# Values of the 16 leading tokens in one layer of a hybrid decoder: from float32 operands, in four column tiles of the array

## The chip, the cores and the metric

The kernel runs on one core of one Trainium2 chip. The metric is the device time of the whole program in microseconds (us), as the median of some runs. A core has a matrix engine (TensorE, PE in the profile), three engines for elementwise work (VectorE or DVE, ScalarE or ACT, GpSimd or POOL), and SyncE (SP), which here only issues transfers. The engines run side by side, each through its own queue in order, and wait for each other on semaphores. Matmul results go to PSUM, which has eight banks.

## What is computed

One layer over 1024 tokens with 16 learned leading tokens (the "meta tokens") ahead of them. One projection of the normed input feeds two groups of heads, a gated delta rule (four heads, in chunks) and softmax attention with a forget gate (eight heads of 64 columns); then come an output projection and a feed-forward block. Cut to what matters:

```python
h = jnp.concatenate([meta, x], axis=1)          # 16 + 1024 tokens
u = rmsnorm(h, attn_norm_w[l])
proj = u @ w_in[l]
gq, gk, gv, gz, gb, ga, fq, fk, fv, ff = jnp.split(proj, IN_SPLITS, axis=-1)
o_gdn = gated_deltanet_group(...)               # gq, gk, gv, gz, gb, ga
o_fox = forgetting_attention_group(fq, fk, fv, ff, fgate_b[l])
h = h + jnp.concatenate([o_gdn, o_fox], axis=-1) @ w_out[l]
h = h + swiglu(rmsnorm(h, ffn_norm_w[l]), w_gate[l], w_up[l], w_down[l])
```

The change touches the rows of `fv` (the attention's values, 512 columns) and `ff` (its eight gate columns) that belong to the 16 leading tokens.

## The kernel before

A float32 product is made of three matmuls in a faster format. `split` (L162 to L165) casts a float32 tile to a high part on ACT (L163) and takes the rest as a low part on DVE (L164); each 128 rows of the contraction are then high by high, high by low and low by high. The normed input lies transposed as `uh` and `ul` (eight slices of 128 channels, 1040 token columns, the leading tokens in the first 16). `win_block` loads a block of the input projection's weights in two halves of four slices each (the raw tile from a pool of two buffers, `wraw`, issued by SP at L175) and splits each half into high and low (from a pool of four buffers each).

PE's order is written out by hand, by `PeOrder` (`od`). Chains of dependent steps, such as `levels` (inverses of the delta rule's triangular blocks), `scan` with its chunks, `csum` and the attention, yield the time at which their next step may come, in a modelled clock `od.t`, which each step advances by what it is charged (`od.pe`). When no chain is due, `od.run` takes one matmul from the fill, a generator: first `fox` (the gate block z0; the values `fv` in two halves of the heads, b=1 and then b=0; the keys `fk`; the queries `fq`), and when that has run out, the first part of the output projection, `wog`. What a fill matmul is charged is its column count divided by 2400. The other engines' queues and SP's are ordered by a scheduler, which simulates the program.

In `fox`, the values take one tile of 128 tokens after another: 24 matmuls through `proj_tmg` into a PSUM bank (three banks take turns, `ps_mm`), then the split into a tile `fvt` (three buffers) with the cast on ACT and the rest on DVE, then a store to `v_d` by SP (L878); for b=1 the eight gate columns are copied to `fr` as well (L881). The 16 leading tokens are the first tile of each half, t=-1: 24 matmuls with 16 stationary columns, `uh` or `ul` of these tokens, and 264 (b=1) or 256 (b=0) weight columns streaming.

While the first half of the values runs, the last delta-rule head is prepared: PE transposes its key norms `rk` (prk, L466 and L467), which come from POOL (L463); DVE copies the row out, SP stores it (L471, L472) and loads it back on all partitions (rkr, L474); DVE and POOL scale the blocks `ktna` (L498 to L502); SP stores them (L504), loads them transposed (`ad`, L543), DVE inverts 32x32 blocks (`up`, L533 and L535) and they go back to memory; `levels` loads the inverses (`ubk`) and copies them into `u` (L610, half on ACT).

At the scan's end each of eight chunks ends in products `po` (L789, L790); ACT copies them to `oc` (L793) and squares them; DVE and POOL make the norm; DVE scales (`on`, L808); PE transposes (`ot`, L814) and `split` writes it for the output projection. Then the attention begins: SP loads for each head its keys and queries (`ka`, `qa`, `kk`, `sa`, L937 to L945) and values (`avt`, L947), and PE makes scores (`sc`, L975 and L976). The memory of these tiles is in part what the scan held until `on` was done.

Of the kernel before, what the change touches and what calls it, by code (L numbers as in the profile page):

```python
# [9 lines left out]
F32 = mybir.dt.float32  # L10
F32R = mybir.dt.float32r
# [4 lines left out]
P = 128  # L16
D = 1024
KT = D // P
NM = 16
S = 1024  # L20
T = NM + S
NT = S // P
GH = 4
FH = 8
DH = 64
# [72 lines left out]
def tile_hymba_layer(ctx, tc, x, meta, attn_norm_w, w_in, conv_w, a_log, dt_bias, gdn_norm_w,  # L98
                     fgate_b, w_out, ffn_norm_w, w_gate, w_up, w_down, final_norm_w, out):
    nc = tc.nc  # L100
# [13 lines left out]
    def ps_mm(name):  # L114
        rot[0] = rot[0] % 3 + 1 if rot[0] else 0
        return ps_v(name) if rot[0] > 1 else bank("mm", 1, name)
# [35 lines left out]
    v_d = dram.tile([FH, T, P], F32, name="v_d")  # L152
# [9 lines left out]
    def split(dst_hi, dst_lo, src):  # L162
        cast = nc.scalar.copy(dst_hi, src)  # L163
        tail[0] = (cast, nc.vector.tensor_sub(dst_lo, src, dst_hi.bitcast(F32)))  # L164
        return cast  # L165

    def load_w(parts, name, hl=None):
        n = sum(m for _, m in parts)
        raw = wraw.tile([P, WMAX], F32, tag="raw", name=f"raw_{name}")
        o = 0  # L170
        for src, m in parts:
            d = raw[:, o:o + m]
            if len(src.shape) == 3:
                d = d.rearrange("p (k c) -> p k c", k=src.shape[1])
            nc.sync.dma_start(d, src)  # L175
            o += m
        hi, lo = hl or (wsp.tile([P, WMAX], F32R, tag=f"w{c}", name=f"w{c}_{name}") for c in ("hi", "lo"))
        for a in range(0, n, n // parts_n[0]):
            b = min(n, a + n // parts_n[0])
            split(hi[:, a:b], lo[:, a:b], raw[:, a:b])  # L180
        return hi, lo

    parts_n = [1]

    def win_block(c0, n, name):
        ws = ([], [])
# [60 lines left out]
    def norm_to(src, rows, wb, hi, lo, col, pool, nm):  # L247
        junk = pool.tile([P, D], F32, tag="junk", name=f"jk_{nm}")
        st = pool.tile([P, 4], F32, tag="st", name=f"st_{nm}")
        with tc.issue_after(casts[-2][0].ins) if len(casts) > 2 else nullcontext():  # L250
            nc.scalar.activation(junk[:rows], src[:rows], AF.Square, accum_out=st[:rows, 0:1])
        pows.append(inv_rms(st[:rows, 2:3], st[:rows, 0:1], 1, 1.0 / D, st[:rows, 1:2]))
        xn = pool.tile([P, D], F32, tag="xn", name=f"xn_{nm}")
        nc.vector.scalar_tensor_tensor(xn[:rows], src[:rows], st[:rows, 2:3], wb[:rows],
                                       op0=ALU.mult, op1=ALU.mult)
        for g in range(2):
            pt = ps_t(f"pt_{nm}_{g}")
            pv = pt.rearrange("p (a b) -> p a b", a=4)[:, :, :rows]
            for i in range(4):
                k = 4 * g + i  # L260
                nc.tensor.transpose(pv[:, i, :], xn[:rows, P * k:P * k + P], ident[:rows, :rows])
            split_dst = (hi[:, 4 * g:4 * g + 4, col:col + rows], lo[:, 4 * g:4 * g + 4, col:col + rows])
            split(split_dst[0], split_dst[1], pv)
        casts.append(tail[0])

    def tok_cols(t):
# [9 lines left out]
    def proj_fm(w, m0, c0, n, name):  # L276
# [2 lines left out]
                          uh[:, k, c0:c0 + n], ul[:, k, c0:c0 + n]) for k in range(KT)])  # L279
        return acc  # L280

    gt = gpool.tile([P, NT + 1, 8], F32, name="gt")
    fr = gpool.tile([P, NT + 1, FH], F32, name="fr")
    nc.gpsimd.memset(gt[:, NT], 0.0)
# [399 lines left out]
    def proj_tmg(acc, t, w, n):  # L684
# [5 lines left out]

    fox_ws = [(GZ, 256, "z0"), (FV + 256, 264, "fv1"), (FV, 256, "fv0"), (FK, 256, "fk0"), (FK + 256, 256, "fk1"),
              (FQ, 256, "fq0"), (FQ + 256, 256, "fq1")]
    fox_w = []

    def fox_load():
        if fox_ws:
            fox_w.append(win_block(*fox_ws.pop(0)))

    def fox_proj(dst, chunks, off, scale, nm):
        for b in range(2):  # L700
# [156 lines left out]
    def fox():  # L857
        fox_load()
        w = fox_w.pop(0)
        for t in range(NT):  # L860
            if t == 1:
                fox_load()
            acc = ps_mm(f"z0_{t}")
            yield from proj_tmg(acc, t, w, 256)
            gate_out(t, acc, fvp, "fvt", 0)
        for b in (1, 0):
            n = 256 + 8 * b
            w = fox_w.pop(0)
            for t in range(-1, NT):
                if t == 1:  # L870
                    fox_load()
                col, rows = tok_cols(t)
                acc = ps_mm(f"fv{b}_{t}")
                yield from proj_tmg(acc, t, w, n)
                vt = fvp.tile([P, 4, 2, DH], F32R, tag="fvt", name=f"fvt{b}_{t}")
                av = acc[:rows, :256].rearrange("p (h d) -> p h d", d=DH)
                split(vt[:rows, :, 0], vt[:rows, :, 1], av)
                nc.sync.dma_start(v_d[4 * b:4 * b + 4, col:col + rows].rearrange("h t d -> t h d"),  # L878
                                  vt[:rows].rearrange("p h a d -> p h (a d)").bitcast(F32))
                if b:  # L880
                    nc.vector.tensor_copy(fr[:rows, NT if t < 0 else t], acc[:rows, 256:264])  # L881
        fvc.close()
        yield from fox_proj(lambda m: k_d[m], TCH, 0, 1.0, "fk")
        od.add(csum(), od.t + 8.0)
        yield from fox_proj(lambda m: q_d[m].rearrange("a p c -> p a c"), ((NM, 342), (NM + 342, 342), (NM + 684, 340)), NM, -DH ** -0.5, "fq")
# [778 lines left out]
```

## Time and profile before

| what | value |
|---|---|
| median of 3 runs | 1319.92 us (1317.76, 1319.92, 1321.94) |
| profiled execution | 1319.71 us, with a span of 1318.0 us |
| mean granted TensorE clock | 0.997 of full |
| values' first half, leading tokens (24 matmuls) | from 235.61 us |
| values' second half, leading tokens (24 matmuls) | from 268.98 us |
| last chunk's products end | 443.79 us |
| first attention scores | 459.99 us |

The profile shows one execution. A line of PE reads: start, duration, engine, line, operation, output <- inputs, shape of the stationary and the streaming operand, count, and in brackets idle time ahead of it with what ended it. In a list of waits the columns are total, times and the longest. A chain of waits goes back from the last instruction through what released each piece.

### The profile page before, as it was taken

Reading aid. Unit: us, or ns where it says so; the run is one execution under the profiler, and the core shown is the slowest. Engines: PE = TensorE matmul, PEld = TensorE weight load, DVE = VectorE, ACT = ScalarE, POOL = GpSimd, SP = SyncE. Lnnn points to the kernel's source line nnn. Section 1 sums busy time; section 2 is a strip of 40 time slices with the busy share of each in tenths; the row PEclk is TensorE's granted clock in tenths of the full one; section 3 lists DMA queues with packets and bytes.
Section 4 is the critical chain, followed back from the end, with each engine's and each line's share of the span. In section 5 each row is a group of like instructions: output and inputs, shape, how many; then the busy total and the mean of one; then the engine's idle time right before and its main releaser. Section 6 shows DMA issues by size and latency. Waiting matters only on the chain.

```text
span 1318.0 us, 20035 instructions
## 1 busy us (share of the span) xinstructions
PE 1294.8 (98%) x7442; PEld 1133.6 (86%) x7442; DVE 855.3 (65%) x1526; ACT 545.4 (41%) x918; POOL 390.8 (30%) x348
## 2 busy tenths in 40 slices
PE   8999999999999999999999999999999999999998
PEld 8999999899999988887777888888888888888887
DVE  6665789676337578996897665566566565355645
ACT  5543434232223367885553232333333343343332
POOL 2211423601013311113432644554334453010301
PEclk9999999999999999999999999999999999999999
DMA  6331743774479597647534555534444557955523
GB/s 227 100 100 45 207 140 112 203 225 148 144 235 323 185 250 219 163 115 228 171 133 137 186 176 184 160 133 157 157 165 155 176 194 264 405 183 180 209 74 128
DMA packets 184776, 233.88 MB, mean 177 GB/s; under 512 B 19120, under 2 KB 136872, under 8 KB 181864
## 3 DMA queue, kind: packets, MB, share of 16 engines
q1 hardware_dynamic: 181704, 223.70, 52.8%
q0 software_dynamic: 2976, 8.92, 2.3%
q8 instruction: 58, 0.95, 0.3%
q14 instruction: 38, 0.31, 0.1%
HBM read 154.91 MB, written 77.67 MB: 176 GB/s over the span
## 4 chain that ended last, share of the span: by engine, by line
PE 74%; DVE 9%; DMA 7%; issue 3%; ACT 3%; SPq 2%; POOL 1%; POOLq 0%; DVEq 0%; ACTq 0%
PE xp L1545 9%; PE yp L1545 7%; PE gb L1379 5%; PE ud L1379 5%; PE gd L1379 5%; PE ub L1379 5%; PE ga L1379 4%; PE ua L1379 4%; PE pj_fk L207 4%; PE pj_fq L207 3%; PE ue L1379 2%; PE ge L1379 2%; PE fv L207 2%; PE pt L1012 2%; PE po L1034 1%
## 5 line engine op out<-in xcount | busy, mean ns | idle before, releaser
L164 DVE TENSOR_TENSOR al_p<-ra_p,ah_p 128x2048 fp32r<-128x2048 f32 (+1 forms) x21 | 46.7, 2222 | 93.7 <-ACT ah_p L163 93.7
L163 ACT CAST ah_p<-ra_p 128x2048 fp32r<-128x2048 f32 (+1 forms) x21 | 37.1, 1766 | 105.8 <-PE xp L1545 48.5
L1545 PE MATMUL xp<-wh_p,al_p 128*128 128x512 f32 (+1 forms) x176 | 67.3, 382 | 0.0
L1545 PE MATMUL xp<-wl_p,ah_p 128*128 128x512 f32 (+1 forms) x176 | 67.3, 382 | 0.0
L1545 PE MATMUL xp<-wh_p,ah_p 128*128 128x512 f32 (+1 forms) x176 | 67.3, 382 | 0.0
L1432 POOL TENSOR_TENSOR gzw<-gzw,uzt 128x512 f32<-128x512 f32 x11 | 18.4, 1673 | 154.9 <-DVE uzt L1423 128.9
L1432 POOL TENSOR_TENSOR gxy<-gxy,uxy 128x512 f32<-128x512 f32 x22 | 38.9, 1766 | 66.1 <-DVE uxy L1423 45.8
L985 ACT ACTIVATE pr<-pr,sm 128x144 f32<-128x144 f32 (+3 forms) x64 | 50.5, 790 | 17.7 <-DVE sm L980 17.4
L1379 PE MATMUL gb<-uh_p,w_g_p 128*128 128x512 f32 x176 | 57.8, 389 | 0.0
L1379 PE MATMUL gd<-uh_p,w_g_p 128*128 128x512 f32 x176 | 57.8, 389 | 0.0
L1379 PE MATMUL ud<-uh_p,w_u_p 128*128 128x512 f32 x176 | 57.8, 389 | 0.0
L1379 PE MATMUL ub<-uh_p,w_u_p 128*128 128x512 f32 x176 | 57.8, 389 | 0.0
L164 DVE TENSOR_TENSOR w_u_p<-raw_u,w_u_p 128x512 fp32r<-128x512 f32 x42 | 42.8, 1018 | 21.6 <-ACT w_u_p L163 21.5
L164 DVE TENSOR_TENSOR pl<-pt,ph 128x512 fp32r<-128x512 f32 (+1 forms) x96 | 51.1, 553 | 2.2 <-ACT ph L163 1.6
L1379 PE MATMUL ga<-uh_p,w_g_p 128*128 128x512 f32 x160 | 52.5, 389 | 0.0
L1379 PE MATMUL ua<-uh_p,w_u_p 128*128 128x512 f32 x160 | 52.5, 389 | 0.0
L1545 PE MATMUL yp<-wh_p,ah_p 128*128 128x512 f32 x132 | 51.3, 389 | 0.0
L1545 PE MATMUL yp<-wl_p,ah_p 128*128 128x512 f32 x132 | 51.3, 389 | 0.0
L1545 PE MATMUL yp<-wh_p,al_p 128*128 128x512 f32 x132 | 51.3, 389 | 0.0
L163 ACT CAST ph<-pt 128x512 fp32r<-128x512 f32 (+1 forms) x96 | 44.9, 471 | 13.8 <-PE pt L1012 13.3
L164 DVE TENSOR_TENSOR wl_p<-rw_p,wh_p 128x2048 fp32r<-128x2048 f32 (+1 forms) x21 | 46.9, 2236 | 3.4 <-ACT wh_p L163 3.4
L163 ACT CAST w_u_p<-raw_u 128x512 fp32r<-128x512 f32 x42 | 26.1, 620 | 52.3 <-PE gd L1379 33.6
(646 smaller groups left out, 4305.4 us busy)
## 6 DMA issues: line engine op xcount, KB each, us to landing
ra_p<-ao_p SPq DMA_DIRECT2D x14, 1024.0 KB
raw_g<-in_w_gate_dram SPq DMA_DIRECT2D x22, 512.0 KB
raw_u<-in_w_up_dram SPq DMA_DIRECT2D x22, 512.0 KB
raw_d<-in_w_down_dram SPq DMA_DIRECT2D x22, 512.0 KB
wt_p<-raw_d SPq DMA_DIRECT2D x33, 256.0 KB
rw_p<-wt_p SPq DMA_DIRECT2D x8, 1024.0 KB
rw_p<-in_w_down_dram SPq DMA_DIRECT2D x6, 1024.0 KB
ao_p<-gzw SPq DMA_DIRECT2D x22, 256.0 KB
```

What stands on the lines that cost most here:

```text
L163: cast = nc.scalar.copy(dst_hi, src)
L164: tail[0] = (cast, nc.vector.tensor_sub(dst_lo, src, dst_hi.bitcast(F32)))
L207: nc.tensor.matmul(dst, a, b, start=first, stop=last)
L985: nc.scalar.activation(pr[:, :n], pr[:, :n], AF.Exp, bias=sm[:, np_ - 1:np_], scale=-1.0, accum_out=rsum[:, h, j:j + 1])
L1012: nc.tensor.transpose(pt[:rows_k, P * j:P * j + P], pts[j][0][:, c0:c0 + rows_k], ident)
L1034: nc.tensor.matmul(po[:, q], vt[:, kt], pl[:, q], start=False, stop=(kt == nk - 1))
L1379: nc.tensor.matmul(dst, a[:, c], b[:, k], start=(first and k == 0 and i == 0), stop=(k == 3 and i == 2), skip_group_check=not first)
L1432: last_mul[0] = G.tensor_tensor(gs[d], gs[d], us[d], op=ALU.mult)
L1545: nc.tensor.matmul(dst[:, n_], a[:, f, c], b[:, f, n_], start=(first and i == 0 and n == 0), stop=(i == NF - 1 and n == 2), skip_group_che ...
```

## The change

The leading tokens' values no longer use the split operands. While the input is normed, a float32 copy of the transposed leading tokens is kept in `xm` (128 channels, eight slices, 32 columns, of which 16 are filled and the rest are zero). A new generator, `fv_meta`, makes the block of each half of the heads ahead of the other tiles: for each of the eight slices, four float32 matmuls with the 32 columns of `xm` stationary and 64 raw weight columns streaming, one for each head, each in its own 32-column tile of the array (`tile_position=(0, 32 * j)`), so that a head's 16 rows come out on partitions 32j to 32j+15. For b=1 the tile j=0 takes 72 columns: its head's and the eight gate columns. The planner is charged 0.12 us for each slice. The result is split as a 128x64 tile, and four stores take the place of one. The weights are read from the raw tiles, so `fox_load` keeps them (`fox_raw`), and the raw tiles are held until `fv_meta` has read them.

```diff
@@ load_w
+        raws_in[:] = [*raws_in[-1:], raw]
         return hi, lo
@@ norm_to
             split(split_dst[0], split_dst[1], pv)
+            if rows < P:
+                nc.vector.tensor_copy(xm[:, 4 * g:4 * g + 4, :rows], pv)
...
+    xm = gpool.tile([P, KT, 32], F32, name="xm")
+    nc.gpsimd.memset(xm, 0.0)
...
+            fox_raw.append(list(raws_in))
+
+    def fv_meta(b, raws):
+        n = 256 + 8 * b
+        acc = ps_mm(f"fvm{b}")
+        for k in range(KT):
+            w = raws[k // 4][:, n * (k % 4):n * (k % 4) + n]
+            for j in range(4):
+                c0, m = (192, n - 192) if j == 0 else (64 * j - 64, 64)
+                nc.tensor.matmul(acc[32 * j:32 * j + 32, :m], xm[:, k], w[:, c0:c0 + m], start=(k == 0),
+                                 stop=(k == KT - 1), tile_position=(0, 32 * j))
+            od.pe(0.12)
+            yield
+        vt = fvp.tile([P, 4, 2, DH], F32R, tag="fvt", name=f"fvmt{b}")
+        split(vt[:, 0, 0], vt[:, 0, 1], acc[:, :DH])
+        for j in range(4):
+            nc.sync.dma_start(v_d[4 * b + (j + 3) % 4, 0:NM],
+                              vt[32 * j:32 * j + NM, 0].rearrange("p a d -> p (a d)").bitcast(F32))
+        if b:
+            nc.vector.tensor_copy(fr[:NM, NT], acc[:NM, DH:DH + 8])
@@ fox
-            for t in range(-1, NT):
+            yield from fv_meta(b, fox_raw[1 if b else 2])
+            for t in range(NT):
...
-                    nc.vector.tensor_copy(fr[:rows, NT if t < 0 else t], acc[:rows, 256:264])
+                    nc.vector.tensor_copy(fr[:rows, t], acc[:rows, 256:264])
```

The change moves instructions beside the block. PE around the transpose prk, where the first half's block ends; before (fv_-1 is the old block, fv_0 the next tile of 128 tokens, tr_v transposes of the delta rule's values):

```order
L207 MATMUL fv_-1_2795<-whi_fv_1_2588,uh 16x264
L207 MATMUL fv_-1_2795<-wlo_fv_1_2589,uh 16x264
L207 MATMUL fv_-1_2795<-whi_fv_1_2588,ul 16x264
L466 MATMUL prk_2326<-ident,rk 8x128
L467 MATMUL prk_2326<-ident,rk 1x16
L437 MATMUL tr_v_0_2382<-ident,vt_1611 128x128 x4
L437 MATMUL tr_v_1_2387<-ident,vt_1611 128x128 x4
L207 MATMUL fv_0_2825<-whi_fv_0_2582,uh 128x264
```

and now (fvm is the new block):

```order
L712 MATMUL fvm_2799<-raw_fv_1_2590,xm 32x64 x2
L471 MATMUL prk_2330<-ident,rk 8x128
L472 MATMUL prk_2330<-ident,rk 1x16
L442 MATMUL tr_v_0_2386<-ident,vt_1615 128x128 x4
L442 MATMUL tr_v_1_2391<-ident,vt_1615 128x128 x4
L712 MATMUL fvm_2799<-raw_fv_1_2590,xm 32x64
L712 MATMUL fvm_2799<-raw_fv_1_2590,xm 32x72
L712 MATMUL fvm_2799<-raw_fv_1_2590,xm 32x64 x3
L208 MATMUL fv_0_2840<-whi_fv_0_2586,uh 128x264
```

The last 5 of the block's 32 matmuls come behind prk and tr_v. (In the changed kernel's own numbering a line is one higher up to L264 of the old, then up to 26 higher.)

ACT in the values' first half, up to the second half's first tiles; before:

```order
L163 CAST fvt_5_3012<-fv_5_2987 128x4x64
L610 COPY u_3364<-ubk_3359 32x16x32
L163 CAST fvt_6_3042<-fv_6_3017 128x4x64
L610 COPY u_3364<-ubk_3359 32x16x32
L163 CAST whi_fk_0_3137<-raw_fk_0_3135 128x1024
L163 CAST fvt_7_3072<-fv_7_3047 128x4x64
L163 CAST whi_fk_1_3143<-raw_fk_1_3141 128x1024
L163 CAST fvt_-1_3102<-fv_-1_3077 16x4x64
```

and now, from three tiles earlier:

```order
L163 CAST fvt_2_2937<-fv_2_2912 128x4x64
L163 CAST whi_fv_0_2872<-raw_fv_0_2870 128x1024
L163 CAST whi_fv_1_2878<-raw_fv_1_2876 128x1024
L163 CAST fvt_3_2967<-fv_3_2942 128x4x64
L163 CAST fvt_4_2997<-fv_4_2972 128x4x64
L163 CAST fvt_5_3027<-fv_5_3002 128x4x64
L163 CAST fvt_6_3057<-fv_6_3032 128x4x64
L615 COPY u_3430<-ubk_3425 32x16x32 x2
L163 CAST fvt_7_3087<-fv_7_3062 128x4x64
L163 CAST fvmt_3125<-fvm_3092 128x64
```

The cast of fvt_6 stands ahead of both copies of `ubk`; the casts of the second half's weights (raw_fv), which stood ahead of the whole first half, are behind fvt_2, and the casts of fk's weights have gone further back. On SP the loads of raw_fv, which were issued long before, stand behind the store of the first half's fvt_0, and raw_fk's first load, which stood there, behind that of fvt_6; the store of the last gate tile (zt_7, L303) stood ahead of the rk row's store (L471) and is now behind `mkv`'s.

DVE at the scan's end; before (on_4936 is the last chunk's output, wlo_wo low parts of the output projection's weights, ul_p the split of a transposed chunk):

```order
L803 TENSOR_TENSOR os_4930<-os_4930,rq_2487 128x4
L212 TENSOR_SCALAR os_4930<-os_4930 128x4
L164 TENSOR_TENSOR ul_p_4148<-ot_4947,uh_p_4146 128x4x128
L805 TENSOR_TENSOR os_4930<-os_4930,rq 128x4
L808 SCALAR_TENSOR_TENSOR on_4936<-oc_4919,os_4930,zt_4851 128x128 x4
L715 SCALAR_TENSOR_TENSOR fhl_fq_358_4963<-pj_fq_358_4907,fhl_fq_358_4963 128x342
L164 TENSOR_TENSOR wlo_wo_10_5799<-raw_wo_10_5796,whi_wo_10_5798 128x512 x2
L164 TENSOR_TENSOR wlo_wo_11_5807<-raw_wo_11_5804,whi_wo_11_5806 128x512 x2
```

and now (on_4990):

```order
L828 TENSOR_TENSOR os_4984<-os_4984,rq_2491 128x4
L164 TENSOR_TENSOR wlo_wo_10_5825<-raw_wo_10_5822,whi_wo_10_5824 128x512
L213 TENSOR_SCALAR os_4984<-os_4984 128x4
L164 TENSOR_TENSOR wlo_wo_10_5825<-raw_wo_10_5822,whi_wo_10_5824 128x512
L164 TENSOR_TENSOR ul_p_4202<-ot_5001,uh_p_4200 128x4x128
L830 TENSOR_TENSOR os_4984<-os_4984,rq 128x4
L164 TENSOR_TENSOR wlo_wo_11_5833<-raw_wo_11_5830,whi_wo_11_5832 128x512
L833 SCALAR_TENSOR_TENSOR on_4990<-oc_4973,os_4984,zt_4905 128x128 x4
L164 TENSOR_TENSOR wlo_wo_11_5833<-raw_wo_11_5830,whi_wo_11_5832 128x512
```

Three of the four wlo_wo casts stand ahead of `on`. They need buffers of the query weights, which are free when fq's last matmuls have read them. On PE at this place, behind the last chunk's products `po`, stood 13 pj_fq, ot of chunk 6, 32 pj_fq, ot of chunk 7, one pj_fq and 36 wog ahead of the first scores; now 13 pj_fq, ot of chunk 6, 10 pj_fq, ot of chunk 7 and 36 wog. On SP one load of raw_wo has moved ahead of the first attention head's loads, and the store of the last-but-one fq tile, which stood behind the first of these loads, ahead of them too.

More of the change, by code (lines that the diff above doesn't have):

```diff
@@ L180, in load_w @@
             split(hi[:, a:b], lo[:, a:b], raw[:, a:b])
+        raws_in[:] = [*raws_in[-1:], raw]
         return hi, lo
-    parts_n = [1]
+    parts_n, raws_in = [1], []
     def win_block(c0, n, name):
@@ L692, in tile_hymba_layer @@
               (FQ, 256, "fq0"), (FQ + 256, 256, "fq1")]
-    fox_w = []
+    fox_w, fox_raw = [], []
     def fox_load():
```

## The prediction

> **What bounds the kernel now.** I read the page first, then what TensorE (PE) waited for, and then the chain that ended last, around the two places where those waits lie. The profiled execution took 1319.71 us: a span of 1318.0 and 1.71 around it. The runs shown have their median at 1319.92, so the profiled one stands for them, and shifts are added to 1319.71. Busy time and the chain by engine, from the page:
>
> ```profile
> PE 1294.8 (98%) x7442; PEld 1133.6 (86%) x7442; DVE 855.3 (65%) x1526; ACT 545.4 (41%) x918; POOL 390.8 (30%) x348
> ...
> PE 74%; DVE 9%; DMA 7%; issue 3%; ACT 3%; SPq 2%; POOL 1%; POOLq 0%; DVEq 0%; ACTq 0%
> ```
>
> PE is busy nearly all the time, but a quarter of the chain is other engines' work: PE work counts only where PE is what is late. PE's waits between 180 and 480 us, longest first:
>
> ```profile
> PE prk L466 <- POOL rk L463: 2.0, 1, 2.0
> PE fv L207 <- DVE up L535: 1.7, 1, 1.7
> PE sc L975 <- DMA qa<-c_d: 1.0, 1, 1.0
> ```
>
> The two blocks that the change replaces stand exactly ahead of the first two waits. PE in order of time (start, duration, shape, and in brackets the wait ahead of it):
>
> ```profile
> 235.61 0.28 PE L207 MATMUL fv_-1_2795<-whi_fv,uh 128*16 128x264 f32 x1
> ...
> 238.38 0.28 PE L207 MATMUL fv_-1_2795<-whi_fv,ul 128*16 128x264 f32 x1
> 240.62 0.27 PE L466 MATMUL prk<-ident,rk 128*8 128x128 f32 x1 [1.96 <-POOL rk L463]
> ...
> 271.62 0.28 PE L207 MATMUL fv_-1_3077<-whi_fv,ul 128*16 128x256 f32 x1
> 273.59 0.36 PE L207 MATMUL fv<-whi_fv,uh 128*128 128x256 f32 x1 [1.69 <-DVE up L535]
> ```
>
> From 240.62 to 271.90 PE works without a wait and still comes 1.69 us too early. So in this stretch PE is not the bound. The chain of waits says what is (start, duration, piece):
>
> ```profile
> 257.83 2.38 POOL ktna L502
> ...
> 261.83 2.67 DMA ad_d<-ktna
> ...
> 265.43 4.59 DMA ad<-ad_d
> ```
>
> That is the preparation of the last delta-rule head: PE's next piece, at 273.59, needs a PSUM bank, which the cast of tile fvt_6 gives back; and on ScalarE (ACT) that cast stands behind a copy at L610 that waits for the end of this preparation:
>
> ```profile
> 271.48 0.62 ACT L610 COPY u<-ubk 32x512 f32<-32x512 f32 x1 [7.37 <-DMA ubk<-ud_d]
> 272.12 0.37 ACT L163 CAST fvt<-fv 128x256 fp32r<-128x256 f32 x1
> ```
>
> From 273.59 on the chain is PE, up to the end of the scan. There it leaves PE again:
>
> ```profile
> 443.79 2.05 PE pj_fq L207 x13
> ...
> 447.99 0.88 DVE on L808 x3
> ...
> 465.31 9.44 DMA ka<-k_d
> ```
>
> The last chunk's output `on` is ready at 447.99+0.88 = 448.87; right after it the loads of the attention heads begin, and head 1's scores wait for them at 476.15:
>
> ```profile
> 451.08 0.60 PE L814 MATMUL ot<-ident,on 128*128 128x128 f32 x4
> ...
> 459.99 0.23 PE L975 MATMUL sc<-ka,qa 70*128 70x144 f32 x1
> ...
> 476.15 0.30 PE L975 MATMUL sc<-ka,qa 70*128 70x144 f32 x1 [0.99 <-DMA qa<-c_d]
> ```
>
> **The change, part by part.**
>
> *The blocks themselves.* Removed: two blocks of 24 matmuls, (238.38−235.61)/23 = 0.120 us apart, 2.9 us each. Added: 32 float32 matmuls each. The trace has float32 matmuls at array positions already: L619 issues 32 for a pair of heads and the trace records 64, so each runs as two passes, and a block has 64. Their pace, from 32 columns and 64 columns (durations of one are min/median/max in ns):
>
> ```profile
> 306.07 2.11 PE L619 MATMUL py<-u,na 32*32 32x32 f32 x64
> ```
> ```profile
> 316.43 0.67 PE L658 MATMUL py<-t 64*64 64x64 f32 x8
> ```
> ```profile
> L619 PE MATMUL py<-u,na x128: 191/191/212, 306.1 to 356.3; 32*32 32x32 f32 x128
> ...
> L658 PE MATMUL py<-t x64: 218/218/267, 316.4 to 371.0; 64*64 64x64 f32 x64
> ```
>
> 32 columns: (2.11−0.19)/63 = 0.030 us a pass; 64 columns: (0.67−0.22)/7 = 0.065. One after another, 64 passes are 4.1 us; if only two column tiles ever overlap, 2.1; at 0.030 each, 2.0. I take 2.1, since the four tiles are meant to overlap and 0.030 is the shortest spacing any row shows. That saves 0.8 us a block, and at both places a wait swallows it: the wait for rk ends when VectorE's and GpSimd's work is done, not PE's.
>
> *Around 240 us.* The order puts 27 of the first block's 32 matmuls ahead of the transpose prk and 5 behind tr_v. PE will wait there 1.96+2.9−1.8 = 3.1 us instead of 1.96. The 5 left over cost 5/32 of 2.1 = 0.3 later. The clock also counts. The stretch after the present wait (columns: length, busy time of PE, its weight loads, DVE, ACT, POOL; then granted clock, DMA share, GB/s):
>
> ```profile
> 240.00:244.00 4.00, 3.38 (x16) 3.23 (x17) 4.00 (x9) 3.12 (x4) 4.00 (x3) 0.61 0.49 64
> ```
>
> A wait of 1.96 us already brought the clock to 0.61 here. The Trainium skill ("TensorE: Matmul & The Clock Gate", Part 1) has the clock fall to half only after an idle window of about 3.4 us; this trace disagrees, with 0.61 after 1.96 us. A lowered clock costs one such stretch about 4.00×(1−0.61) = 1.6 us of PE work, now hidden by the 1.69 us wait.
>
> *The end of the preparation.* Two things let it end earlier. SyncE's queue no longer has the gate store L303 ahead of the rk row's store, which now waits for it:
>
> ```profile
> 244.99 0.34 SPq L303 DMA_DIRECT2D rec_d<-zt  x1
> 245.43 0.28 SPq L471 DMA_DIRECT2D rk_d<-rkt  x1
> ```
>
> and VectorE idles 3.27 us for the row that comes of it, just ahead of ktna:
>
> ```profile
> 255.44 0.16 DVE L522 TENSOR_TENSOR ems<-ems,rkr 16x16 f32<-16x16 f32 x1 [3.27 <-DMA rkr<-rk_d]
> ```
>
> And the cast of fvt_6 now stands ahead of the copies at L610. So PE may start the second half's tiles as soon as it gets there: 271.90−0.8+0.3 = 271.4, 2.2 us earlier than 273.59. Bounds for this gain g: nothing, if the longer wait at 240 keeps the clock down for a second stretch (−1.6) or the store's landing holds the bank; 2.2 at most. I take 1.7, nearer to the upper end, since both causes of the wait are gone from the order.
>
> *Moved or small.* The second half's weights (raw_fv) are loaded at the place in SyncE's queue where raw_fk stood, 252 us, and cast ahead of fvt_3. Between that cast and the next use of its bank lie two tiles of PE work, 24×0.120 = 2.9 us each, so a late landing costs nothing up to some 3 us, and past that each us counts. The two copies into xm, its memset, six more small stores and the narrower split go at nothing: VectorE, GpSimd and SyncE have idle time in these stretches, as the 3.27 us row shows for VectorE.
>
> *The end of the scan.* The planner charges each block 0.96 us where it charged about 2.6, so it hands out the fill earlier relative to the chains: behind the last chunk's products stand 23 pj_fq matmuls instead of 46. One takes 2.05/13 = 0.158, so the last products come 23×0.158 = 3.6 us later, less g, while the work left behind them is shorter by as much. What hangs on these products is late by that. Worse, VectorE's queue now has the first wlo_wo cast of part 11 ahead of `on`:
>
> ```profile
> 449.42 1.15 ACT L163 CAST whi_wo<-raw_wo 128x512 fp32r<-128x512 f32 x2 [1.25 <-PE pj_fq L207]
> ```
> ```profile
> 447.72 1.14 DVE L808 SCALAR_TENSOR_TENSOR on<-oc,os,zt 128x128 f32<-128x128 f32 x4
> ...
> 450.07 1.29 DVE L164 TENSOR_TENSOR wlo_wo<-raw_wo,whi_wo 128x512 fp32r<-128x512 f32 x2 [0.79 <-ACT whi_wo L163]
> ```
>
> It needs a buffer that the last-but-one pj_fq matmul frees. Counted from the end of the last products: 22 pj_fq and one ot (0.45) are 3.9 us; one whi_wo 0.6, one wlo_wo 0.65, `on` 1.14, some 0.15 of hand-over: 6.45. Before it was 448.87−443.79 = 5.08. PE gets to the last ot after 23×0.158+0.45 = 4.1 and waits 2.4 us, which is new. The first scores follow ot by 459.99−451.08−0.16 = 8.75, so they come at 6.5+8.75 = 15.25 behind the products instead of 16.2: net 3.6−0.95−g = 2.7−1.7 = +1.0 us. If the clock falls after the new wait as it did after 1.96 us, +2.6. By the skill's page it would not fall, and +1.0 stands.
>
> Head 1's scores wait for loads that follow `on`: these start 3.6+1.4−g = 5.0−1.7 = 3.3 us later. Some comes back, since one store no longer stands behind `on`, and one of the two raw_wo loads goes ahead of it:
>
> ```profile
> 449.57 0.57 SPq L717 DMA_DIRECT2D q_d<-fhl_fq  x1
> ...
> 471.50 0.94 SPq L175 DMA_DIRECT2D raw_wo<-in_w_out_dram  x2
> ```
>
> 0.57+0.94/2 = 1.0 us of SyncE's time; between 0 and 2 with what their bytes took from the others. So head 1's scores move by 3.3−1.0 = +2.3, more than the first scores, and from there PE is the bound again. The sum: 1319.71+2.3 = 1322.0 us.
>
> **The rivals.** *Scan end at full price.* g is 0 to 0.5 because the longer wait at 240 holds the clock down, and the loads give nothing back: 5.0−0.25 = +4.8, 1324.5. It decides from g and relief together under 0.8 (5.0−0.8 = 4.2 us above). For it: DMA is what ends the wait at 476.15, and the clock row. Against: the store moved ahead in the order.
>
> *PE alone decides.* The loads have slack that the chain doesn't show, `on` isn't held, and the clock doesn't fall at 240, as PE's wait now lies elsewhere in time: −1.7 (g), −1.6 (clock), −0.99 (wait at 476.15): 1315.4. For it: PE's 98%. Against: the chain runs through `on` and the loads.
>
> *The column tiles run one after another*, so the change doesn't do what it says: 4.1 us a block. The second is then 1.3 us longer than before, and the 5 left over cost 0.6: PE arrives at 271.90+1.3+0.6 = 273.8, g = −0.2, and the scan's end adds 5.0+0.2−1.0: +4.2, 1323.9.
>
> **How the numbers follow.** A measurement of this kernel tells about 0.3%, 4 us, from no change; "same" is 1315.8 to 1323.9. Forecast 0.50, its own range from +1.0 (the first scores' shift, if the loads give back all) to +4.2 (g 0.8 and nothing given back): 1320.7 to 1323.9, all same. Full price 0.22, slower. PE alone 0.15, faster. One after another 0.13, on the edge: 0.10 slower, 0.03 same. Together: faster 0.15, same 0.53, slower 0.32. The range leaves out the lower rival and the last bit of the upper: 1316.5 to 1324.8.
>
> **What would show it.** Right: 32 matmuls of a block within 2 to 2.3 us, PE's wait for rk near 3 us, none ahead of the second half's first tile, a new wait of about 2.4 us ahead of the last ot for DVE's `on`, and a longer wait than 0.99 us ahead of head 1's scores. Wrong: blocks of 4 us; a wait left at the second half's first tile; casts of raw_fv that hold fvt_3; the last ot without a wait; or head 1's loads landing as long before PE as now.

## The result and the profile after

Seven runs of the changed kernel have their median at 1326.57 us (1321.79 to 1331.50), against 1319.92 before (seven runs): a ratio of 1.0057, with a 95% interval of 1.0041 to 1.0072. The kernel became slower, by more than the range on record allowed for (up to 1324.8). The profiled execution took 1326.06 us, 6.35 above that of before. One execution of e5 in the table further down, of 4517.9 us, is left out of its median.

What PE waited for in the changed kernel, the longest first:

```profile
PE prk L471 <- POOL rk L468: 4.0, 1, 4.0
PE sc L1001 <- issue: 2.2, 1, 2.2
...
PE ot L839 <- DVE on L833: 1.7, 1, 1.7
PE fv L208 <- DVE fvt L164: 1.4, 1, 1.4
```

The wait for rk has doubled. The wait ahead of the second half's first tile (1.69 before) is gone, but a new one of 1.4 stands in the same half. At the scan's end there is the new wait ahead of the last `ot`, and the one ahead of head 1's scores (`sc`) has grown from 0.99. PE at the first two places:

```profile
235.48 1.06 PE L712 MATMUL fvm<-raw_fv,xm 128*32 128x72 f32 x54
240.55 0.38 PE L471 MATMUL prk<-ident,rk 128*8 128x128 f32 x1 [4.01 <-POOL rk L468]
...
270.66 1.10 PE L712 MATMUL fvm<-raw_fv,xm 128*32 128x64 f32 x64
271.69 0.39 PE L208 MATMUL fv<-whi_fv,uh 128*128 128x256 f32 x1
...
281.87 0.39 PE L208 MATMUL fv<-whi_fv,uh 128*128 128x256 f32 x1 [1.42 <-DVE fvt L164]
```

A block of 64 passes takes 1.10 us instead of 2.9: all four column tiles run at once. Behind the longer wait for rk the granted clock (the column behind POOL's) stays down for a second stretch of 4 us. The changed kernel:

```profile
240.00:244.00 4.00, 3.45 (x22) 2.69 (x23) 2.71 (x9) 3.19 (x4) 4.00 (x4) 0.51 0.38 50
244.00:248.00 4.00, 4.00 (x24) 3.73 (x23) 0.54 (x4) 0.00 (x0) 3.84 (x6) 0.63 0.70 170
```

Before, the first of these stretches had 0.61, and the second was nearly free:

```profile
244.00:248.00 4.00, 4.00 (x32) 3.82 (x32) 1.19 (x5) 0.37 (x1) 3.84 (x4) 0.96 0.37 108
```

Worked out as 4 us times what is missing from 1.00, this costs 3.4 us instead of 1.7, and PE comes to the second block at 270.66, 1.7 us later than before. The shorter block more than makes up for it: the second half starts at 271.69, 1.9 us earlier than before. At its fourth tile (281.87) this gain is used up. SyncE's queue says why (start, duration of the issue, transfer), and ACT the same from the other side:

```profile
268.39 5.55 SPq L608 DMA_DIRECT2D na<-rec_d  x4
274.04 2.27 SPq L904 DMA_DIRECT2D v_d<-fvt  x1
```
```profile
268.05 0.37 ACT L163 CAST fvt<-fv 128x256 fp32r<-128x256 f32 x1 [2.78 <-DMA v_d<-fvt]
271.73 1.25 ACT L615 COPY u<-ubk 32x512 f32<-32x512 f32 x2 [3.31 <-DMA ubk<-ud_d]
...
280.99 0.37 ACT L163 CAST fvt<-fv 128x256 fp32r<-128x256 f32 x1 [2.91 <-DMA v_d<-fvt]
```

The cast of fvt_6 came at 268.05, 4.1 us earlier than before, since it no longer stands behind the copy of `ubk`. That copy itself, the end of the last head's preparation, came no earlier (271.73, before 271.48). DVE had fvt_6's low part ready at 270.88, but the store had to wait for the issue of four loads of `na` and left at 274.04. Before, with three of these loads ahead of it and the fourth between two stores, it left at nearly the same time (274.18, the last of these lines):

```profile
267.88 3.65 SPq L603 DMA_DIRECT2D na<-rec_d  x3
271.63 1.53 SPq L878 DMA_DIRECT2D v_d<-fvt  x1
273.21 0.87 SPq L603 DMA_DIRECT2D na<-rec_d  x1
274.18 1.68 SPq L878 DMA_DIRECT2D v_d<-fvt  x1
```

By the chain of waits of the changed kernel the store landed 6.85 us after its issue began:

```profile
274.04 6.85 DMA v_d<-fvt
```

The first tile of the second half takes the buffer that this store gives back, so its cast (280.99) was held, and with it the PSUM bank that the fourth tile needs. The scan's end, from the same chain:

```profile
447.56 2.00 PE pj_fq L208 x13
...
452.74 1.25 DVE on L833 x4
...
462.98 9.26 DMA avt<-v_d
...
472.74 7.21 DMA ka<-k_d
```

The last products end at 447.56, 3.8 us later than before. `on` is ready at 453.99, 6.43 us behind them. Head 1's scores come at 481.51, 27.5 us behind `on` (27.3 before). SyncE comes to the load `avt` sooner behind `on`, 9.0 us instead of 10.2, but by the chain the next load waits for that transfer, 9.26 us long; before, it was 5.71:

```profile
459.09 5.71 DMA avt<-v_d
```

Behind each of the two waits of PE the granted clock is down in the changed kernel:

```profile
452.00:456.00 4.00, 2.77 (x11) 2.02 (x12) 3.64 (x9) 1.51 (x4) 3.15 (x6) 0.89 0.52 158
456.00:460.00 4.00, 4.00 (x14) 3.19 (x13) 0.69 (x1) 0.00 (x0) 2.83 (x6) 0.68 0.74 234
480.00:484.00 4.00, 2.48 (x10) 2.24 (x11) 1.40 (x6) 0.94 (x4) 1.10 (x2) 0.81 1.12 337
484.00:488.00 4.00, 4.00 (x25) 3.44 (x25) 2.92 (x10) 2.52 (x8) 0.54 (x1) 0.77 1.05 161
```

Worked out in the same way, these are 1.7 us at each place.

### The profile page after: what moved, and what is told of

It reads as the page before. It is cut to its first block, busy times and chain, and to the rows that moved or that the text cites. A ratio compares the mean times of both kernels' runs of the same rounds, so it can differ in the third digit from the quotient of the medians.

```text
span 1324.3 us, 20205 instructions
## 1 busy us (share of the span) xinstructions
PE 1294.8 (98%) x7522; PEld 1133.2 (86%) x7522; DVE 859.0 (65%) x1528; ACT 545.4 (41%) x918; POOL 388.1 (29%) x349
## 4 chain that ended last, share of the span: by engine, by line
PE 76%; DVE 7%; DMA 7%; issue 4%; ACT 3%; POOL 1%; SPq 1%; POOLq 0%; DVEq 0%; ACTq 0%
PE xp L1571 8%; PE yp L1571 7%; PE gb L1405 5%; PE ud L1405 5%; PE gd L1405 5%; PE ub L1405 5%; PE ua L1405 4%; PE ga L1405 4%; PE pj_fq L208 3%; PE ue L1405 2%; PE ge L1405 2%; PE pj_fk L208 2%; PE fv L208 2%; PE pt L1038 2%; PE po L1060 1%
```

## The experiments

For all profiles, three stretches between starts of PE instructions tell where the time went. A goes from the first half's leading-token block to the first key product (`pj_fk`), B from there to the last pair of products `po`, C from there to the last scores (`sc`). All in us, one profile each; the last columns are the median of the runs and the ratio to the kernel before, run on the same chip, with its interval. The medians of before on these chips lie between 1318.39 and 1319.92, so rows are to be compared by the ratio. In e7 the first block stands earlier in the order, and its A is not like the others.

| kernel | A | B | C | median | ratio |
|---|---|---|---|---|---|
| before | 60.7 | 147.1 | 147.1 | 1319.92 | |
| changed | 61.0 | 150.7 | 150.0 | 1326.57 | 1.0057 (1.0041 to 1.0072) |
| e1, old charge | 61.9 | 148.2 | 146.9 | 1323.08 | 1.0033 (1.0021 to 1.0045) |
| e2, old block, new charge | 60.9 | 151.1 | 151.6 | 1329.49 | 1.0077 (1.0056 to 1.0098) |
| e3, `on` first | 62.9 | 150.4 | 151.0 | 1330.22 | 1.0088 (1.0063 to 1.0112) |
| e4, na late, old charge | 61.3 | 148.7 | 146.9 | 1324.31 | 1.0028 (1.0012 to 1.0045) |
| e5, `on` and loads first | 62.5 | 150.3 | 150.3 | 1330.56 | 1.0088 (1.0059 to 1.0118) |
| e6, more fill left | 60.2 | 144.5 | 151.2 | 1322.12 | 1.0026 (1.0015 to 1.0037) |
| e7, blocks early, old charge | (73.5) | 148.6 | 146.5 | 1327.20 | 1.0072 (1.0052 to 1.0092) |
| e8, no column tiles | 63.4 | 152.9 | 145.9 | 1327.14 | 1.0077 (1.0056 to 1.0097) |
| e9, changed again | 62.4 | 150.3 | 150.3 | 1329.25 | 1.0074 (1.0059 to 1.0088) |
| e10, busy at scores | 62.1 | 150.5 | 146.8 | 1327.99 | 1.0069 (1.0050 to 1.0087) |
| e11, busy at both | 63.5 | 150.3 | 148.2 | 1327.47 | 1.0064 (1.0049 to 1.0080) |
| e12, late fk1 | 62.4 | 147.9 | 146.6 | 1321.50 | 1.0021 (1.0007 to 1.0034) |
| e13, late fk1 and na | 58.3 | 150.3 | 146.3 | 1320.57 | 1.0012 (0.9997 to 1.0027) |

The row of the changed kernel against that of before: A +0.3, B +3.6, C +2.9. B is the planner's: 23 times 0.158. C should have been shorter by the same 3.6, since 23 products less are left in it, and is longer by 2.9. So waits and clock in C cost 6.5 us.

**e1 and e2: the charge and the block, apart.** e1 is the changed kernel with the old charge, e2 the old block with the new one:

```diff
-            od.pe(0.12)
+            od.pe(3 * n / 2400)
```
```diff
-                                          w[1][k][:, :n]) for k in range(KT)], n / 2400)
+                                          w[1][k][:, :n]) for k in range(KT)], 0.04 if t < 0 else n / 2400)
```

> The changed kernel, with the planner charged for a block as for the old one (8 times 3n/2400, 2.64 and 2.56 us) instead of 8 times 0.12. The new blocks, their loads and their stores stay; at the scan's end 46 pj_fq stand behind the last products again, as before, and no wlo_wo cast ahead of the last chunk's output. Theory (the loss is the order at the scan's end, which the planner's charge brings about): within 1.5 us of the kernel before, 1318.5 to 1321.5, with the last ot not waiting and about 1 us of wait ahead of head 1's scores. Rival (the loss is the block and what it moves at 235 to 285 us: the 4 us wait for rk, the clock, the held raw weights): the time stays near 1326.

> The kernel before, with the old blocks of 24 matmuls, but the planner charged 0.04 us for each of their matmuls, 0.96 us a block, as the change does. At the scan's end 23 pj_fq stand behind the last products and three wlo_wo casts ahead of the last chunk's output, as in the changed kernel; the new block, its loads and its stores aren't there. Theory (order at the scan's end): slower than before by 4 to 6.5 us, 1324 to 1326.5. Rival (the block): the time before, 1319 to 1321.

e2 has nothing of the change but the planner's charge, and loses 0.77%, some 10 us. Its PE waits between 400 and 500 us:

```profile
PE sc L975 <- DMA vmt<-v_d: 4.8, 1, 4.8
PE ot L814 <- DVE on L808: 1.7, 1, 1.7
```

B is 4.0 longer and C 4.5, as the theory has it; the loss is larger than expected because the wait at head 1's scores, 4.8 us, and the clock behind it came on top. e1 takes that order back: C is as before, and so is the order at the scan's end. But e1 is not as fast as before, 0.21 to 0.45% slower, where the theory had allowed 1.5 us. So a second loss exists, outside the scan's end. In its profile it lies in A (+1.3) and in one wait of 1.0 us for a chunk's load in B:

```profile
PE fv L208 <- DVE fvt L164: 1.9, 1, 1.9
...
PE p L787 <- DMA ra<-rec_d: 1.0, 1, 1.0
```

The rest of e1's difference in that profile, 1.6 us, lies ahead of the block and is not the same in other profiles.

**e3 and e5: the casts ahead of the last output.** e3 issues the low parts of the second output weight block behind the last `on` (an ordering rule around the subtraction in `split`); e5 adds an order on GpSimd (the last two lines):

```diff
+            lo_after[0] = last_on[0] if nb else None
             wvs[nb] = wout_block(0, nb)
+            lo_after[0] = None
...
+                with tc.issue_after(last_qa[0].ins):
+                    nc.gpsimd.memset(masks[0], 0.0)
```

> The changed kernel, with the low parts of the output projection's second weight block issued behind the last chunk's output on DVE, as before; the 23 pj_fq stay. Theory: of the 5.1 us by which the last output is late, 1.4 are the casts' and 3.6 the fill's: the output is ready 5.1 us behind the last products instead of 6.4, PE's wait ahead of the last ot falls from 1.7 to about 0.5, and the time falls by 1.4 us, or up to 2.5 if the clock then stays up: 1324 to 1325.5. Rival (the casts alone are the loss): near 1320 to 1321. Rival (the block): unchanged, 1326.

> As e3_on_first, and GpSimd's mask for the attention made behind the ones and minus ones of the attention's ka and qa, as before, instead of ahead of them. In e3_on_first the last output was ready 5.2 us behind the last products, as expected, yet the loads stood still until 458.6 us, because GpSimd's mask step, 0.29 us in the changed kernel, took 2.64 us beside four casts on DVE. Theory (head 1's scores follow the loads, and these the last output and ka's ones): the scores of head 1 come 3 to 4 us earlier than in e3_on_first against the same last products, and the time is 1 to 2.5 us under the changed kernel, 1324 to 1325.5. Rival (the loads are held by something else): as e3_on_first, 1328 to 1330.

In e3 `on` was ready 5.2 us behind the products instead of 6.4, as expected, and PE's wait ahead of the last `ot` fell to 0.55. The time did not fall. GpSimd and DVE at that place:

```profile
455.02 2.64 POOL L991 TENSOR_SCALAR_AFFINE_SELECT zmask<-zmask 128x128 f32<-128x128 f32 x1
457.62 0.96 POOL L947 MEMSET ka<- 6x1040 f32 x1
```
```profile
455.01 2.49 DVE L165 TENSOR_TENSOR wlo_wo<-raw_wo,whi_wo 128x512 fp32r<-128x512 f32 x4
```

The mask step (`zmask`), 0.29 us in the changed kernel, lasted as long as DVE's four casts beside it, and the attention's `ka` and its loads waited for it. Here and below "casts" on DVE are the subtractions that make the low parts. The Trainium skill ("SBUF — State Buffer", Who interferes with whom) has DVE and GpSimd share one pair of memory ports as an exclusive lock; these rows agree, with 2.64 us for 0.29. In e5 only the filling of `ka` and `qa` stands beside the same four casts, and it takes its usual 0.96 and 0.94 us. There the mask comes later, the loads follow `on` at once, and head 1's scores come 27.7 us behind it, where e3 needed 29.9. That part of the theory held (2.2 us; 3 to 4 were expected). But the time, 1330.56, did not come down to 1324 to 1325.5: PE arrives sooner and waits 3.65 us at head 1's scores instead of 2.2, and the clock behind that wait is lower. The casts' 1.2 us (6.4 against 5.2) are real in the chain and are not what decides the time.

**e4, e12 and e13: what the values' two halves lose.** e4 is e1 with the `na` loads issued behind the first half's last value store. e12 is e1 with the keys' second weight block loaded behind the second half's last value store. e13 is both, with the second pair's `na` behind the last store, too (from its edit; like e4 and e12 it has e1's charge as well):

```diff
+            with tc.issue_after((v_all[15] if hp else v_st[-1]).ins):
                 nc.sync.dma_start(na[:, i], rec_d[:, :, 0, 2 * hp + i].rearrange("t p c -> p t c"))
...
+            ld_after[0] = v_all[15] if fox_ws[0][2] == 'fk1' else None
             fox_w.append(win_block(*fox_ws.pop(0)))
```

> As e1_old_charge, and the loads of the scaled blocks na for the triangular inverses (four of 512 KB) issued behind the store of the first half's last value tile instead of ahead of the store of fvt_6. Theory (the 1.9 us by which the second half of the values starts earlier are lost at its fourth tile, since a store of fvt_6 waits in SyncE's queue for these loads): the fourth tile doesn't wait, and the time is 1.5 to 2 us under e1_old_charge, 1317 to 1319. Rival (that start is no longer on the path, the scan is paced by something else): as e1_old_charge.

> As e1_old_charge, with the raw weights of the keys' second block (two loads of 512 KB) issued behind the last value store instead of from 284 us on, among the value stores. Theory (the value tiles wait for stores, the stores for the transfers that now lie among them): from the first block of the leading tokens to the first key product 60.5 to 61.5 us, instead of 61.9 in e1_old_charge and 62.3 in the mean of seven such profiles, and the time 0.5 to 1.5 us under e1_old_charge, 1321.5 to 1322.5. Rival (the stores wait for something else): no change there, 1323.

> As e12_late_fk1, and the loads of na (four of 512 KB) behind the first half's last value store, for the second pair of heads behind the second half's. Theory: that stretch takes 58.5 to 60 us, less than the 60.7 before, since PE's 3.6 us of saved work and the earlier start of the second half are kept at last, and the time is 1318 to 1320, at or below before. Rival (the scan's end and the attention take up what is gained here, as in e6_more_fill): the stretch is shorter and the time still 1321 to 1323.

e4 keeps more of the early start up to the fourth tile, which comes 44.7 us behind the first block, where e1 has 46.2 and the changed kernel 46.4. But at the seventh tile PE waits 2.1 us: the four loads of `na`, issued from 276.94 now, hold SyncE's queue as long as they did before, and the second half's first store waits behind them and a load of fk1's weights. The time is that of e1, as the rival had it.

```profile
276.94 5.53 SPq L609 DMA_DIRECT2D na<-rec_d  x4
282.57 1.57 SPq L175 DMA_DIRECT2D raw_fk<-in_w_in_dram  x1
284.23 1.35 SPq L907 DMA_DIRECT2D v_d<-fvt  x1
```

e12 alone does not shorten A in its profile (62.4), against the theory. Its median lies on the edge of the expected range, but its ratio can't be told from e1's, so the hit proves nothing. e13 holds back both loads of fk1's weights and half of the `na` loads, and A falls to 58.3, 2.4 us less than before. SyncE in e13, two loads of `na` between the value stores instead of four, and no weights of fk1:

```profile
273.81 1.87 SPq L724 DMA_DIRECT2D v_d<-fvmt  x4
275.73 1.05 SPq L611 DMA_DIRECT2D na<-rec_d  x2
278.64 16.86 SPq L911 DMA_DIRECT2D v_d<-fvt  x8
295.55 2.08 SPq L176 DMA_DIRECT2D raw_fk<-in_w_in_dram  x2
```

So with these loads out of the way the gain that the prediction counted on is there in the profile. The time of e13, a little above the 1318 to 1320 expected, can't be told from before (0.9997 to 1.0027): its B is 3.2 us longer. Of this, 0.5 is a wait in the triangular steps, 0.7 a wait for a chunk's load, and 1.7 the clock, which fell behind the first of them:

```profile
320.00:324.00 4.00, 4.00 (x16) 4.00 (x17) 3.90 (x10) 0.46 (x1) 2.38 (x3) 0.58 0.49 152
```

It is the only version here with the new block that keeps up with the kernel before; none beats it. Whether a gain in A is always taken back in B, or by chance in this profile, is not shown.

**e6: more fill left for the scan's end.** The kernel before, with the planner charged twice for the old block:

```diff
-                                          w[1][k][:, :n]) for k in range(KT)], n / 2400)
+                                          w[1][k][:, :n]) for k in range(KT)], (2 if t < 0 else 1) * n / 2400)
```

> The kernel before, with the planner charged twice for the old blocks (5.28 and 5.12 us): 81 pj_fq stand behind the last products instead of 46, so that these come 35 times 0.158, 5.5 us, earlier. Theory (the scan's end sets when the attention's loads begin, and the kernel before is still 1 us late there): the wait of about 1 us ahead of head 1's scores goes, and the time is 0.5 to 1.5 us under before, not more, since PE is the bound again: 1318 to 1319.5. Rival (the loads set the pace of the attention further on, too): 3 us or more under before. Rival (the products come no earlier): as before.

The wait at head 1's scores went, as expected, but the kernel was 0.26% slower where 0.5 to 1.5 us less were expected. The products came 2.4 us earlier instead of 5.5, since now the scan waits for its own steps:

```profile
PE p L762 <- DVE s L783: 1.7, 1, 1.7
PE p L762 <- DMA ra<-rec_d: 0.7, 1, 0.7
```

Of the three counts tried, 46 products left behind the scan is the best: 23 cost some 9 to 10 us (e2), 81 cost 2 to 3.

**e7: the blocks moved forward.** e1 with the first block ahead of the seventh gate tile, the second ahead of the first half's third tile:

```diff
+            if t == 6:
+                yield from fv_meta(1, fox_raw[1])
             acc = ps_mm(f"z0_{t}")
...
+                if b and t == 2:
+                    yield from fv_meta(0, fox_raw[2])
                 acc = ps_mm(f"fv{b}_{t}")
-            yield from fv_meta(b, fox_raw[1 if b else 2])
```

> As e1_old_charge, with the two new blocks moved forward in the fill: the first half's ahead of the seventh gate tile, the second half's ahead of the third tile of the first half, so that the raw weights are free sooner, raw_fv is loaded ahead of the rk row's store and raw_fk ahead of the values' first stores, and neither block stands ahead of a wait of PE. Theory (e1_old_charge lost its 3.5 us to loads and stores in the stretch from 250 to 290 us, which the held raw weights moved there): back to before or below it, 1317 to 1320. Rival (float32 tiles or the long wait for rk with its clock are the loss): as e1_old_charge, 1323.

The theory failed here: the wait for rk went (0.3), and waits of 1.6, 2.1, 2.6 and 4.4 us for DVE took its place. The first key product came at 303.13, 6.9 us later than before. So taking away PE's wait at 240 us does not shorten this stretch; why DVE came so late here was not followed up.

**e8: no column tiles.** The changed kernel with 8 matmuls of all columns for a block, and with the split and the single store of the kernel before:

```diff
-            for j in range(4):
-                c0, m = (192, n - 192) if j == 0 else (64 * j - 64, 64)
-                nc.tensor.matmul(acc[32 * j:32 * j + 32, :m], xm[:, k], w[:, c0:c0 + m], start=(k == 0),
-                                 stop=(k == KT - 1), tile_position=(0, 32 * j))
+            nc.tensor.matmul(acc[:NM, :n], xm[:, k, :NM], w, start=(k == 0), stop=(k == KT - 1))
```

> The changed kernel, with each block as 8 float32 matmuls of all 264 or 256 columns with 16 stationary columns, not in four column tiles; split and store as before the change. The raw weights are still read and held, and the planner charged 0.12 for each of the 8. Theory (the time of a block is hidden, and the order is what costs): the block takes 16 passes of 0.27, about 4.3 us, instead of 1.1, and the time stays within 1.5 us of the changed kernel, 1325 to 1328. Rival (the column tiles' 1.1 us count): 3 us or more above the changed kernel.

```profile
236.00 3.73 PE L710 MATMUL fvm<-raw_fv,xm 128*16 128x264 f32 x16
```

3.73 us instead of 1.06, and the time, 1327.14, is that of the changed kernel within its interval. The block's own length makes no difference that can be seen. (The scheduler placed prk and the first tile's matmuls otherwise here, with a wait for rk of 0.4 us, so A and B aren't like for like.)

**e9, e10 and e11: the clock.** e9 is the changed kernel once more; e10 puts 11 idle products ahead of head 1's first scores, e11 8 more ahead of the last `ot`, in the PSUM tile that is then overwritten:

```diff
+                for _ in range(11 if (h, j, i) == (1, 0, 0) else 0):
+                    nc.tensor.matmul(sc[:, :P], ident, ident, start=True, stop=True)
```

> The changed kernel itself, once more, beside the two below: 1325 to 1328, and a second profile of the stretch from 235 to 300 us. There the first profile shows the values' first half ending 0.2 us later than before, where e1_old_charge and e3_on_first, with the same order of the engines in this stretch, ended it 1.3 and 2.2 us later against their own start; theory: this profile, too, shows a loss of 0.2 to 2.5 us there and no gain.

> The changed kernel with 11 idle products of the identity with itself (about 2.4 us) in the PSUM bank of head 1's first scores, ahead of these, where PE waits 2.2 us for the head's loads. Nothing else moves. Theory (the clock falls after that wait, and costs 1.3 to 1.7 us of the attention's start): the clock stays at full from 480 to 490 us, and the time is 0.5 to 1.7 us under e9_changed_again. Rival (the clock costs nothing, the attention waits for its loads anyway): as e9_changed_again or up to 0.5 above.

> As e10_busy_at_scores, and 8 such products (about 1.8 us) ahead of the last chunk's transposes, where PE waits 1.7 us for the last output. Theory (both falls of the clock count): full clock from 452 to 460 us as well, the first scores 1.5 us earlier, and 1.5 to 3 us under e9_changed_again, if head 1's scores don't wait for the loads by as much more; if they do, as e10_busy_at_scores. Rival as there.

e9 shows the loss in A again (1.7 us); its time is above the 1325 to 1328 expected. The clock behind head 1's first scores, e9 and then e10:

```profile
480.00:484.00 4.00, 2.55 (x9) 2.18 (x10) 0.85 (x4) 0.77 (x3) 1.10 (x2) 0.59 1.10 337
484.00:488.00 4.00, 4.00 (x20) 3.56 (x19) 2.82 (x9) 1.83 (x6) 0.54 (x1) 0.55 1.05 200
```
```profile
480.00:484.00 4.00, 4.00 (x32) 3.66 (x31) 2.08 (x9) 1.64 (x6) 0.18 (x1) 1.00 1.08 365
484.00:488.00 4.00, 4.00 (x30) 3.68 (x29) 3.42 (x10) 3.63 (x10) 2.77 (x5) 1.00 1.07 213
```

With PE kept busy the clock stays up, and stretch C is 3.5 us shorter, 146.8 instead of 150.3 (148.2 in e11). The times go the expected way, 1.3 us under e9 (e10) and 1.8 (e11), but their intervals overlap e9's, so that size is not settled by them. In e9, e10 and e2 the clock stayed at 1.00 from 452 to 460 us although the wait ahead of the last `ot` was 1.69 us as in the changed kernel's first profile; in e8 it fell again, to 0.5. That fall comes in some executions and not in others, and what e11 adds there could not be seen.

## Why the prediction was wrong, point by point

- *The block is hidden.* As far as e8 can tell, right: it stretches the block to 3.7 us and the time stays. Its length, taken as 2.1, was 1.06 to 1.10 us: 64×0.065/4 = 1.04, four tiles at once. The Trainium skill ("TensorEngine Tiling (Array Packing)", Theoretical Speedup) gives up to four times for a dimension of at most 32; e8's 3.73 against 1.06 is 3.5. The rival of tiles that run one after another is out.
- *The gain g at the second half.* The step that failed: "I take 1.7, nearer to the upper end, since both causes of the wait are gone from the order." Of the causes only the order of fvt_6's cast worked: the row's store did leave 1.2 us earlier, but the preparation ended no sooner. (The bank that PE waited for is given back by DVE's low part, which follows the cast: 273.37 before, 270.88 now.) PE did start 1.9 us earlier, at 271.69 where 271.4 was expected, but that was luck in part: the block saved 1.9 us instead of 0.8, and the clock, which stayed down for a second stretch as one of the bounds had it, took 1.7 more. Then the first tile needs a buffer whose store queues behind the `na` loads, as many as before and now in one row, and beside loads of weights that have moved there. A was 0.3 us longer in the profile, and 1.2 to 2.8 longer in e1, e3, e5 and e9 to e12. So g was not 1.7 but nothing; the bound that the prediction named, a store's landing, was the value to take. The clock's second stretch is not what decides: in e10 the clock fell for one stretch only (0.66, then 0.91) and A was 62.1. e13 shows 2.4 us that were to be had.
- *The scan's end.* The mechanism was right, and the terms were close: products late by 23×0.158 = 3.6 (3.8 with g at zero), `on` 6.45 behind them (6.43), the first scores 15.25 behind the products without a fall of the clock (14.9 to 15.1 in e2 and e9 to e11; 16.5 in the changed kernel's first profile, with the fall), a new wait ahead of the last `ot` (2.4 expected, 1.7). e2 shows that the planner's charge alone brings all of this. The first scores came 4.1 us later than before, not 1.0: g was missing, and the clock fell.
- *The relief of 1.0 us* for head 1's loads did not come: they need 27.5 us behind `on`, 27.3 before. SyncE did reach `avt` 1.2 us sooner, and lost it to that transfer. Single profiles scatter by more than this term: 26.0 us in e10, 26.7 in e9, 28.7 in e2.
- *The clock.* Mis-sized: a fall was counted only as a possibility at the first scores, and none behind head 1's wait. In the profile both came, 1.7 us each. The first is hidden, since PE waits for head 1's loads behind it anyway; the second is not.
- So the sum was 5.0 − 0 − 0 = +5.0 at head 1's scores (5.4 measured), and +1.0 behind it: close to the rival "scan end at full price" (+4.8), with the clock on top. It had a chance of 0.22. Its loss of g was to come from the clock at 240 us, though, and came from the stores.

What stays open: the two losses don't add up. The order alone (e2) costs 0.56 to 0.98%, the block with the old order (e1) 0.21 to 0.45%, and both together (changed and e9) 0.41 to 0.88%. The runs of all versions with the new block scatter over 3 to 14 us, those of before over 4 to 10, and the profiles show single waits of 1 to 3 us with the clock behind them that come in some and not in others, as at the output projection, where e9's two waits are 2.6 us together and the changed kernel's one 1.1. How much of a loss is such chance was not separated. The loss of the block with the old order (e1) has its cause in part argued: e13 takes away loads between the stores and, by the medians, most of the loss, but the intervals of the two overlap (1.0021 to 1.0045, 0.9997 to 1.0027).

## What to carry to other kernels

In a kernel whose order comes from a planner's clock, the charge of a step is part of the change: a step made cheaper moves all fill behind it, and here that cost more (9 to 10 us in e2) than both blocks ever took (5.8). Ahead of a gain that a cast or a start brings forward, read the queue of the stores that free its buffers, to the last load that stands in it. Price a new wait of PE with the clock behind it, not by its length alone.

## What the runs showed of the hardware

- Float32 matmuls with 32 stationary and 64 streaming columns in four column tiles: 64 passes in 1.10 us, 0.017 each, against 0.065 for passes one after another at the same columns, and 3.73 us for 16 passes of 264 columns.
- The granted clock fell to half, for one or two stretches of about 3.4 us (read in steps of 0.2 us), behind every wait of PE of more than 2.2 us between 200 and 700 us in these profiles. Behind waits of 1.7 to 2.2 us it fell in some (2.16 and 1.69 in the changed kernel, 1.96 in the kernel before) and not in others (2.20 in e2, 2.13 in e4, 1.69 in e2, e9 and e10). It fell behind 0.5 us (e13) and 0.9 us (e8) among small triangular matmuls. The Trainium skill ("TensorE: Matmul & The Clock Gate", Part 1) names an idle window of about 3.4 us that runs free; the falls behind shorter waits disagree with its length, and that one and the same wait falls or not agrees with a window that runs free.
- Four loads of 512 KB held SyncE's queue for 5.55 us (5.53 in e4), and a store behind them that was ready at 270.88 left at 274.04.
- GpSimd's mask step took 2.64 us beside four subtractions on DVE, 0.29 without them; its fills beside the same subtractions took their usual 0.96 us (e5).
